# A two-layer trunk on one core: the FFN's down product summed in PSUM, and a unit's decays and first low-rank stage put behind the preceding unit's inversion

## The chip, the cores and the metric

The kernel runs on one core of a Trainium2 chip. The metric is the device time of one execution in microseconds (us). A core has engines that run their own instruction streams: TensorE (PE) for matrix products, VectorE (DVE), ScalarE (ACT) and GpSimd (POOL) for elementwise work, and SyncE (SP), which here issues the transfers (DMAs) between HBM and on-chip memory. PE writes its results to PSUM, of which the kernel uses eight banks of 128x512 fp32 numbers; the other engines read them there.

## The reference, cut to what matters

The program is a trunk of two layers over 1024 tokens of width 1024, all in float32. Each layer has a mixer and a gated FFN, both with a residual and a LayerNorm after it. The mixer of layer 0 is RWKV-7, a recurrence over time; that of layer 1 is sparse attention (called dsa in the code).

```python
def _wkv7_step(state, inp):
    r_t, w_t, k_t, v_t, a_t, b_t = inp
    sa = jnp.einsum('bhvk,bhk->bhv', state, a_t)
    state = (state * w_t[:, :, None, :] + sa[..., None] * b_t[:, :, None, :]
             + v_t[..., None] * k_t[:, :, None, :])
    y = jnp.einsum('bhvk,bhk->bhv', state, r_t)
    return state, y
...
w_log = -jax.nn.softplus(-(w0 + jnp.tanh(xw @ w1) @ w2)) - 0.5      # low-rank
decay = jnp.exp(-jnp.exp(w_log.astype(f32)))
a = jax.nn.sigmoid(a0 + (xa @ a1) @ a2)                              # low-rank
g = jax.nn.sigmoid(xg @ g1) @ g2                                     # low-rank
...
def conv_ffn(x, w_up, conv_w, conv_b, w_down):
    u = x @ w_up                                                     # 1024 -> 5632
    up = jnp.pad(u, ((0, 0), (CONV_W - 1, 0), (0, 0)))
    u = sum(up[:, j:j + S] * conv_w[j] for j in range(CONV_W)) + conv_b
    gate, val = jnp.split(u, 2, axis=-1)
    return (jax.nn.silu(gate) * val) @ w_down                        # 2816 -> 1024
...
for i in range(DEPTH):
    ...
    x = layer_norm(DN_ALPHA * x + h, ln_g[i, 0], ln_b[i, 0])
    f = conv_ffn(x, ffn_w_up[i], ffn_conv_w[i], ffn_conv_b[i], ffn_w_down[i])
    x = layer_norm(DN_ALPHA * x + f, ln_g[i, 1], ln_b[i, 1])
```

## The kernel before, in words

A float32 product is made of three matmuls on rounded operands (mm3, lines 65 to 67): each operand is split into a high part, which ACT casts (line 54), and a low part, the rest, which DVE or POOL subtracts (line 60). High by high, low by high and high by low are summed in the same PSUM bank.

The program runs in five stretches: the RWKV mixer (to about 960 us), the FFN of layer 0 (its up product to 1437.8 us, its down product to 1733 us, where dsa's first transposes begin), dsa (to about 2430 us), and the FFN of layer 1 (up to 2893.1 us, down to the end at 3168.0 us). A scheduler places each instruction on its engine's stream from the order in which the code issues it and from when its inputs come ready; `tc.issue_after(i)` keeps the instructions issued inside it behind instruction `i` on that instruction's own engine.

**RWKV.** There are four units (hf, g): token half hf and head half g, units 0 to 3. For each unit the stages are low-rank products (lora1 at line 401, once for each hf, and lora2 at 497), projections (kproj, rproj, vproj; PSUM tiles "pa"), decays (510), prep (603), bonus (579), the inversion of the chunks' triangular matrices (invert, 630) and the recurrence over eight chunks (wkv, 695). In the inversion DVE runs a chain of 30 steps on the tile Lt, each a product (line 644, into ltmp) and a sum (line 650), and then transposes the result (lines 655 and 660), on which PE works (lines 667 and 672). In wkv every chunk goes round PE (ups at 718, dps at 724) and DVE (the copy UV at 719, the state S at 727), so that a chunk waits for the one before. `CFG['order']` is a list of stages with an offset: x is the loading of the next token half with lora1, l lora2, d decays, b bonus, i invert, w and W the first and second four chunks, and the digit says how many units ahead. Decays are, for each of four head pairs, one scan (520), one difference (521) and one product on DVE (527), and some work on ACT and POOL. lora1 is, for each of eight k tiles, a difference (406) and three scaled sums on DVE (413), and four matmuls.

**The down product.** It multiplies hd (2816 features by 1024 tokens, stored in HBM by the gating) by w_down (2816 by 1024). The features are cut into 22 tiles f of 128, in 11 pairs p. Of the first 20 features (layer 0) or 18 (layer 1) the product is made by Strassen's and Winograd's scheme: token halves, column halves and the two f of a pair are the 2x2 blocks, and seven products (`11`, `12`, `S1`, `S2`, `S3`, `S4`, `22`) take the place of eight. Pairs are taken in groups (`cuts`, 4 in layer 0, 3 in layer 1): d_load brings hd and w_down of a group's pairs, d_op makes the sums of operands on DVE (lines 908 and 1147) and splits them (dh, dl; 128x1024 at a time), `down` makes the 128x512 products for four token tiles tt, summed in PSUM over a group's pairs, and add_to (line 1166) adds each bank to the sums acc in SBUF, on DVE. The last two f (layer 0) or four (layer 1) are the "tail": a direct product "dt" (line 1260) for each token tile and column half, added to acc, after which norm_store normalizes the tile's rows and stores them. In layer 0 dsa's first steps are interleaved with the tail: two blocks of 32 small matmuls (wqk, line 1326), the stores of what ACT and POOL make of them, and the loads of x for dsa's transposes (line 1357).

Of the kernel before, what the change touches and what calls it, by code (L numbers as in the profile page):

```python
# [300 lines left out]
CFG = {'order': 'k0 r0 a0 A0 v0 x1 l0 l1 x0 d0 b0 i0 w0 W0 r1 d1', 'da': 'p', 'db': 'p', 'kk': 'p', 'uv': 'a', 'go': 'v', 'gz': 'p', 'wr': 'pppv', 'wk': 'vp', 'wv': 'pv', 'xl': 'ppp', 'xp': 'vppppppp', 'p1': 'q0 w q5 i4 t1 at i5', 'n1': 27, 'n2a': 26, 'n2b': 19, 'n3': 20, 'n4': 12, 'qp': 2, 'lag': 2, 'cm': 'pppp', 'phc': 'aaaa', 'olc': 'a', 'qm': 'av', 'quq': 'p', 'quk': 'v', 'sh': 16, 'tc': 'a', 'kve': 'a', 'cB': 'a', 'cU': 'a', 'cY': 'a', 'cV': 'aaaa', 'cR': 'aaaa', 'cT': 'a', 'cM': 'a', 'cUV': 'v', 'sq': 'a', 'kkE': 'a', 'pfl': 'n', 'l2': 'v', 'l1': 'v', 'wo0': 'vppvppvp', 'wl': 'ppvv', 'wl2': 'v', 'wl3': 'vv', 'gz2': 'v', 'yq': 'a', 'pfo': 0, 'pf0': 0, 'pf1': 1, 'pf2': 2, 'dwo0': 'pppppppp', 'dwl': 'vvvv', 'dwl2': 'v', 'dwl3': 'vv', 'tke': 'av', 'rt': 'f2 l0 z f0 f1 p0 p2 l1 f3 p1 p3 p4 l2 l4 l5 l3', 'dt': 'l0 a z l1 p0 p4 p2 p3 p1 l5 l2 l3 l4', 'eT1': 'pvpvvvpv', 'eT3': 'pvpvpppv', 'fs0': 'x0 x1 y1 y0 x2 y2 x3 y3 r0 r1 u0 r3 u3 r2 u4 u6 u2 u7 u5 u1', 'fs1': 'x0 y0 x1 x3 y1 x2 y2 r0 u0 y3 r1 r2 u1 r3 u3 u4 u2 u5 u6 u7', 'eT2': 'vvvvvvvv', 'e22': 'vvvvvvvv', 'eR': 'vvvvvvvv', 'tkp': 'vv', 'kvs': 1, 'ln0': 'pp', 'ln1': 'vv', 'ln2': 'pppppppv', 'ln3': 'pppppppv', 'ln4': ['pp', 'pp'], 'gl': 2, 'ga': '0g1g', 'dl0': 'pppppvppp'}  # L301
# [5 lines left out]
def rwkv(k, src, dst):  # L307
# [201 lines left out]

    def decays(hf, g):  # L510
# [4 lines left out]
        with tc.issue_after(s["last"].ins):  # L515
# [114 lines left out]
    def invert(hf, g):  # L630
# [21 lines left out]
        for sub in range(2):  # L652
# [5 lines left out]
            for b in range(2):  # L658
                q = slice(64 + 32 * b, 96 + 32 * b)
                nc.vector.transpose(  # L660
                    L[q, :, 32 * b : 32 * b + 32].rearrange("p n i -> p i n"),
                    Lt[64 * sub + 32 * b : 64 * sub + 32 * b + 32],
                )
            for o in (0, 16):
# [172 lines left out]
    def stage(n, i):  # L837
# [3 lines left out]
        if n == "x":  # L841
            if un_[1] == 0:
                load_x(un_[0])
                lora1(un_[0])
# [39 lines left out]
def ffn(k, layer, src, dst):  # L884
# [239 lines left out]
    NPAIR = NF // 2  # L1124
    cuts = [0, 3, 6, 8, 10] if layer == 0 else [0, 3, 6, 9]
    groups = [range(a, b) for a, b in zip(cuts, cuts[1:])]
# [849 lines left out]
```

## The time and the profile before

| | |
|---|---|
| time before, median of 3 runs | 3173.01 us (3172.37 to 3178.31) |
| the profiled execution's own time | 3170.01 us |
| its span in the profile | 3168.0 us |
| PE busy | 2834.0 us (89%) |
| DVE busy | 2463.5 us (78%) |
| POOL busy / ACT busy | 1528.7 us (48%) / 1368.9 us (43%) |
| granted PE clock, mean | 0.937 |

A row of grouped instructions has line, engine, operation, output and inputs, shape and count, then busy time and the mean of one, then the engine's idle time just before them and what ended it. A row of the timeline has start, duration, engine, line, operation and count, and in brackets the idle time before it with what ended it. A matmul's duration there (0.39 us) is its latency; matmuls follow each other faster than that. The view by windows gives for a stretch the busy time of PE, PE's weight loads, DVE, ACT and POOL with their counts, the granted PE clock (1.00 is full), the busy share of the DMA engines and GB/s.

### The profile page before, as it was taken

The page shows a single profiled execution, that of the slowest core. Times are in us where ns is not written, and L with a number is a line of the kernel's source. Part 1 is how long each engine was busy: PE and PEld are TensorE (multiplying, and loading weights), DVE is VectorE, ACT ScalarE, POOL GpSimd, SP SyncE. Part 2 cuts the span into 40 slices and gives each one's busy share as a digit, 9 for nine tenths or more (in the row PEclk, how much of TensorE's full clock was granted, in tenths as well). Part 3 has the DMA queues.
Part 4 walks back from the last instruction along what each step waited for, and adds up shares of the span by engine and source line. Part 5 has one row for each costly group of instructions (what it writes and reads, how often), then busy time and mean ns, then how long its engine had stood idle before and what let it go on. Part 6 is the DMA issues. An engine that isn't in the chain of part 4 may idle for free. (4 is left out here: it accounts for less than half of the span.)

```text
span 3168.0 us, 41686 instructions
## 1 busy us (share of the span) xinstructions
PE 2834.0 (89%) x15032; PEld 2217.4 (70%) x15032; DVE 2463.5 (78%) x3911; ACT 1368.9 (43%) x2353; POOL 1528.7 (48%) x987
## 2 busy tenths in 40 slices
PE   7789998898988999997888888889998899998798
PEld 3577576786866777775667765667776677777577
DVE  6776776768576888889786699995675888888965
ACT  4433243322233544443224487784363444444231
POOL 3525045140246666666677222212214666666766
PEclk9889998898998999998998989899999999999899
DMA  6645435344162222244115221113224222225212
GB/s 214 246 152 195 142 121 199 134 148 146 64 201 89 80 80 80 80 143 189 41 40 173 102 90 37 34 40 115 77 66 151 60 80 80 80 81 206 80 53 93
DMA packets 235232, 354.87 MB, mean 112 GB/s; under 512 B 17194, under 2 KB 110762, under 8 KB 234642
## 3 DMA queue, kind: packets, MB, share of 16 engines
q1 hardware_dynamic: 221202, 327.04, 31.6%
q10 hardware_dynamic: 13824, 25.17, 2.2%
q8 instruction: 118, 1.93, 0.3%
q14 instruction: 88, 0.72, 0.1%
HBM read 248.99 MB, written 103.15 MB: 111 GB/s over the span
## 5 line engine op out<-in xcount | busy, mean ns | idle before, releaser
L60 POOL TENSOR_TENSOR wo<-wr,wo 128x512 fp32r<-128x512 f32 x220 | 414.3, 1907 | 289.4 <-ACT wo L54 289.4
L1039 DVE SCALAR_TENSOR_TENSOR cv<-u,vec,cv 128x1023 f32<-128x1023 f32 (+1 forms) x176 | 348.0, 1995 | 52.9 <-ACT cv L1034 51.2
L65 PE MATMUL dn<-dh 128*128 128x512 f32 x532 | 220.3, 414 | 67.8 <-DVE acc L1166 67.8
L60 POOL TENSOR_TENSOR dl<-raw,dh 128x1024 fp32r<-128x1024 f32 x82 | 220.2, 2708 | 102.2 <-ACT dh L54 96.7
L65 PE MATMUL p<-xT,wo 128*128 128x512 f32 x528 | 213.1, 404 | 27.8 <-ACT u L1023 18.2
L66 PE MATMUL dn<-dl,dh 128*128 128x512 f32 x532 | 218.1, 410 | 14.3 <-DVE dl L60 7.5
L1671 POOL TENSOR_TENSOR cm<-sc,toep 128x256 f32<-128x256 f32 x96 | 75.7, 795 | 298.1 <-DVE mn L1687 229.7
L1034 ACT ACTIVATE cv<-u,vec 128x1024 f32<-128x1024 f32 x88 | 109.5, 1244 | 250.2 <-DVE u L1028 249.6
L67 PE MATMUL dn<-dh,dl 128*128 128x512 f32 x532 | 217.0, 408 | 0.0
L67 PE MATMUL p<-xT,wo 128*128 128x512 f32 x528 | 208.8, 395 | 2.9 <-POOL wo L60 2.9
L66 PE MATMUL p<-xT,wo 128*128 128x512 f32 x528 | 208.5, 395 | 3.0 <-DVE xT L60 3.0
L1166 DVE SCALAR_TENSOR_TENSOR acc<-acc,dn 128x512 f32<-128x512 f32 x196 | 131.0, 680 | 86.3 <-PE dn L67 86.3
L60 POOL TENSOR_TENSOR wo<-S,wo 128x512 fp32r<-128x512 f32 x88 | 173.3, 1987 | 30.0 <-ACT wo L54 25.7
L54 ACT CAST dh<-raw 128x1024 fp32r<-128x1024 f32 x95 | 94.8, 1047 | 199.6 <-issue 81.1
L65 PEld LDWEIGHTS dn<-dh 128*128 128x128 f32 x532 | 106.3, 200 | 98.5 <-DVE acc L1166 42.2
L60 POOL TENSOR_TENSOR wl<-wr,wh 128x512 fp32r<-128x512 f32 x56 | 76.3, 1363 | 181.7 <-ACT wh L54 109.1
L65 PEld LDWEIGHTS p<-xT,wo 128*128 128x128 f32 x528 | 100.7, 191 | 65.4 <-ACT u L1023 33.0
L65 PE MATMUL p<-x,wo 128*128 128x512 f32 x352 | 138.9, 394 | 3.4 <-DVE x L60 3.0
L54 ACT CAST wo<-wr 128x512 fp32r<-128x512 f32 x220 | 127.2, 619 | 27.3 <-POOL wo L60 18.6
L67 PE MATMUL p<-x,wo 128*128 128x512 f32 x352 | 138.4, 393 | 0.0
L66 PE MATMUL p<-x,wo 128*128 128x512 f32 x352 | 138.4, 393 | 0.0
L66 PEld LDWEIGHTS dn<-dl,dh 128*128 128x128 f32 x532 | 106.5, 200 | 38.4 <-DVE dl L60 8.4
(412 smaller groups left out, 8552.0 us busy)
## 6 DMA issues: line engine op xcount, KB each, us to landing
wr<-in_w_up_dram SPq DMA_DIRECT2D x88, 512.0 KB, 5.9
hd<-cv SPq DMA_DIRECT2D x44, 512.0 KB, 3.4
raw<-hd SPq DMA_DIRECT2D x19, 1024.0 KB, 5.0
raw<-in_w_down_dram SPq DMA_DIRECT2D x19, 1024.0 KB, 7.6
wr<-in_w_wo_dram SPq DMA_DIRECT2D x68, 256.0 KB, 2.9
wr<-in_w_rkv_dram SPq DMA_DIRECT2D x48, 256.0 KB, 4.3
kept_w<-wh ACTq DMA_DIRECT2D x48, 256.0 KB, 3.5
kept_w<-wl SPq DMA_DIRECT2D x48, 256.0 KB, 3.0
```

What stands on the lines that cost most here:

```text
L54: nc.scalar.copy(hi, raw)
L60: eng.tensor_tensor(lo, raw, f32(hi), ALU.subtract)
L65: mm(ps, lhs[0], rhs[0], start=start, stop=False, **kw)
L66: mm(ps, lhs[0], rhs[1], start=False, stop=False, **kw)
L67: mm(ps, lhs[1], rhs[0], start=False, stop=stop, **kw)
L1034: nc.scalar.activation(o, u, AF.Identity, bias=k.vec[:, cb : cb + 1], scale=k.vec[:, cw[2] : cw[2] + 1])
L1039: nc.vector.scalar_tensor_tensor(o[:, d:], u[:, : 1024 - d], k.vec[:, cw[j] : cw[j] + 1], o[:, d:], ALU.mult, ALU.add)
L1166: nc.vector.scalar_tensor_tensor(o, o, ALPHA if first else 1.0, ps, ALU.mult, ALU.add)
L1671: (nc.vector if CFG["cm"][h4] == "v" else nc.gpsimd).tensor_tensor(cm[:, :near], mk, toep[g][:, h % 8, 256 - near :], ALU.add)
```

## The change

The **down product** becomes a direct one. It runs over two token halves hf and eleven pairs p in 22 steps. d_prep of a step loads the half's 512 tokens of hd for the pair (hr, 512 KB) and both rows of w_down (dr, 2 x 512 KB), and splits them: three 128x1024 casts on ACT, the low part of hd on DVE (on POOL in the second half of layer 1 for four pairs), both low parts of w_down on POOL. It is issued two steps ahead. A step has 48 matmuls: two f, three products, four token tiles, two column halves. All eight banks of a half stay open over its eleven pairs; the last two pairs are done bank by bank in d_end, with one addition of the bank to the residual rows on DVE, and after it d_norm. w_down is read and split for each half. The Strassen products, their operand sums, the 196 additions of banks to acc (111 of them in layer 0) and the tail product are gone. d_norm of the first half lies in the middle of the product; in layer 0 dsa's first steps are interleaved with d_end of the second half.

The **recurrence** changes in its order only: in `CFG['order']` x1 and l1 stand behind i0, not ahead of l0, and decays and lora1 are issued inside `tc.issue_after` of the last transpose of the first half of the preceding unit's inversion. What is computed there is the same.

```diff
-CFG = {'order': 'k0 r0 a0 A0 v0 x1 l0 l1 x0 d0 b0 i0 w0 W0 r1 d1',
+CFG = {'order': 'k0 r0 a0 A0 v0 l0 x0 d0 b0 i0 x1 l1 w0 W0 r1 d1',
...
+    inverted = []
+
     def decays(hf, g):
...
-        with tc.issue_after(s["last"].ins):
+        with tc.issue_after(s["last"].ins), tc.issue_after(inverted[-1].ins) if inverted else nullcontext():
...
-                nc.vector.transpose(
+                tr = nc.vector.transpose(
                     L[q, :, 32 * b : 32 * b + 32].rearrange("p n i -> p i n"),
                     Lt[64 * sub + 32 * b : 64 * sub + 32 * b + 32],
                 )
+            if sub == 0:
+                inverted.append(tr)
...
-                lora1(un_[0])
+                with tc.issue_after(inverted[-1].ins) if inverted else nullcontext():
+                    lora1(un_[0])
...
+    NPAIR, LAST = NF // 2, 2
+    ops, hold, lnw, sums, rows = {}, {}, [], {}, {}
+
+    def d_prep(hf, p):
+        late = hf == 1 and p >= NPAIR - LAST
+        hr = t4("hr")
+        nc.sync.dma_start(
+            hr.rearrange("p (f c) -> p f c", f=2), hd[p][:, :, 512 * hf : 512 * hf + 512].rearrange("f p c -> p f c")
+        )
...
+        split(k, hr, *h, "a", "p" if layer and hf and p < 4 else "v")
+        for f in range(2):
+            wr = t4("dr", pool=N_)
+            nc.sync.dma_start(wr, k.w_down[layer, (2 * p + f) * 128 : (2 * p + f + 1) * 128, :])
+            split(k, wr, w[:, 2 * f], w[:, 2 * f + 1], "a", "p")
+        ops[hf, p] = *h, w
+
+    def d_mm(ps, hf, p, tt, ch):
+        hh, hl, w = ops[hf, p]
+        for f in range(2):
+            ts = slice(512 * f + 128 * tt, 512 * f + 128 * tt + 128)
+            cs = slice(512 * ch, 512 * ch + 512)
             mm3(
+                k, ps, (hh[:, ts], hl[:, ts]), (w[:, 2 * f, cs], w[:, 2 * f + 1, cs]), p == f == 0,
+                p == NPAIR - 1 and f == 1,
             )
+
+    def d_end(ps, hf, tt, ch):
+        for p in range(NPAIR - LAST, NPAIR):
+            d_mm(ps, hf, p, tt, ch)
...
+        nc.vector.scalar_tensor_tensor(
+            r, r, ALPHA, ps, ALU.mult, ALU.add, accum_out=sums[hf, tt][:, ch : ch + 1]
+        )
+
+    def d_norm(hf, tt):
...
+    steps = [(hf, p) for hf in range(2) for p in range(NPAIR)]
+    for s in steps[:2]:
+        d_prep(*s)
+    for f in range(NF - CFG["gl"], NF):
+        gated(f)
+    order = [(ch, tt) for ch in (1, 0) for tt in range(4)]
+    for i, (hf, p) in enumerate(steps):
+        if i + 2 < len(steps):
+            d_prep(*steps[i + 2])
+        if p == 0:
+            bk = {x: bank("dn", PX if x[0] == 0 else PY) for x in order}
+        if p < NPAIR - LAST:
+            for ch, tt in order:
+                d_mm(bk[ch, tt], hf, p, tt, ch)
...
+        if (hf, p) == (0, NPAIR - 1):
+            for ch, tt in order:
+                d_end(bk[ch, tt], 0, tt, ch)
+                if ch == 0:
+                    d_norm(0, tt)
+    for tt in range(4):
+        d_end(bk[1, tt], 1, tt, 1)
     if layer == 0:
         pools.close(P_, N_, PY)
         yield
...
+    for tt in range(4):
+        d_end(bk[0, tt], 1, tt, 0)
+        d_norm(1, tt)
         if layer == 0:
             yield
```

The streams show three places that the diff does not. The first is DVE in the inversion of unit 0, in the second half of the chain on Lt. Before, rows of decays (520, 521, 527) and a low part of a weight (wl) stand between the steps:

```order
L644 TENSOR_TENSOR ltmp<-Lt 128x220
L650 TENSOR_TENSOR Lt<-Lt,ltmp 128x11x20
L520 SCALAR_TENSOR_TENSOR c<-smask,BK 128x512
L644 TENSOR_TENSOR ltmp<-Lt 128x210
L60 TENSOR_TENSOR wl<-wr,wh 128x512
L650 TENSOR_TENSOR Lt<-Lt,ltmp 128x10x21
L521 TENSOR_TENSOR d<-c,BK 128x512
L644 TENSOR_TENSOR ltmp<-Lt 128x198
L650 TENSOR_TENSOR Lt<-Lt,ltmp 128x9x22
L527 TENSOR_TENSOR BK<-AR,ip 128x8x64
```

In the changed kernel (where 644, 650, 655, 660 and 719 of before are 647, 653, 658, 663 and 724) the chain's steps stand alone up to the transposes, and the decays follow:

```order
L647 TENSOR_TENSOR ltmp<-Lt 128x30
L653 TENSOR_TENSOR Lt<-Lt,ltmp 128x30
L658 STREAM_TRANSPOSE TX<-Lt 32x32x32
L663 STREAM_TRANSPOSE MA<-Lt 32x32x32 x3
L658 STREAM_TRANSPOSE TX<-Lt 32x32x32
L663 STREAM_TRANSPOSE MA<-Lt 32x32x32
L523 SCALAR_TENSOR_TENSOR c<-smask,BK 128x512
L524 TENSOR_TENSOR d<-c,BK 128x512
L724 COPY UV<-ups 64x512
```

So the twelve DVE instructions of the unit's decays moved from between the chain's steps to between the steps of wkv's chunks; the first copy UV of wkv has two of them ahead of it. Unit 2 reads the same.

The second place is DVE in unit 1, where lora1 of the second token half stood in the middle of the chain (ahead of its step on 128x238). Of the changed kernel:

```order
L663 STREAM_TRANSPOSE MA<-Lt 32x32x32
L406 TENSOR_TENSOR xx<-xT 128x512 x2
L413 SCALAR_TENSOR_TENSOR xm<-xx,vec,xT 128x512 x6
L406 TENSOR_TENSOR xx<-xT 128x512 x2
L413 SCALAR_TENSOR_TENSOR xm<-xx,vec,xT 128x512 x6
L406 TENSOR_TENSOR xx<-xT 128x512 x2
L413 SCALAR_TENSOR_TENSOR xm<-xx,vec,xT 128x512 x6
L406 TENSOR_TENSOR xx<-xT 128x512 x2
L413 SCALAR_TENSOR_TENSOR xm<-xx,vec,xT 128x512 x6
L724 COPY UV<-ups 64x512
```

All 32 instructions of lora1 now stand behind the inversion and ahead of the first copy UV of the unit's recurrence, and on PE the matmuls of lora1 stand between ups and dps of that first chunk.

The third place is the end of layer 0's down product, on SP and PE. On SP (x_4 to x_6 are stores of normalized rows, wqkh and wqkl those of wqk, xr the loads of x for dsa's transposes) the changed kernel has, with rows that repeat left out:

```order
L1295 DMA wqk<-wqkh 128x512
L1295 DMA wqk<-wqkl 128x512
L1280 DMA uk<-in_w_uk_dram 128x512
L149 DMA x_4_78<-acc 128x512 x2
L149 DMA x_5_79<-acc 128x512
L149 DMA x_6_80<-acc 128x512
L1304 DMA grow<-in_dsa_rows_dram 128x512
L1271 DMA xr<-x_0_74 128x512 x2
```

Eight stores of wqk stand ahead of the second load of uk, the other eight between x_4 and grow, all ahead of the loads xr. Before, SP had these kinds in the same order, with the rows x_0 to x_2 where x_4 to x_6 are now. What moved is the work of PE beside them. Where PE had these rows around its second block of wqk before,

```order
L67 MATMUL dt<-to 128x512
L1326 MATMUL wqk<-uk,uq 128x128 x16
L65 MATMUL dt<-to 128x512
L66 MATMUL dt<-to 128x512
```

it now has

```order
L66 MATMUL dn<-wd,hl 128x512
L1287 MATMUL wqk<-uk,uq 128x128 x16
L67 MATMUL dn<-wd,hl 128x512
L65 MATMUL dn<-wd,hl 128x512
```

Between the two blocks of wqk stood 45 matmuls and stand 34; between the second block and dsa's transposes stood 39 and stand 10.

More of the change, by code (lines that the diff above doesn't have):

```diff
@@ L1121, in ffn @@
             gated(f)
-    NPAIR = NF // 2
-    cuts = [0, 3, 6, 8, 10] if layer == 0 else [0, 3, 6, 9]
-    groups = [range(a, b) for a, b in zip(cuts, cuts[1:])]
-    in_P = (0, 3, 4, 8, 9) if layer == 0 else (0, 3, 6, 8)
-    tail = range(2 * cuts[-1], NF)
-    acc = []
-    R = {}
-    def d_load(p):
-        r = R[p] = dict(raw=big("raw", P_ if p in in_P else L_, (128, 8, 512), F32))
-        raw = r["raw"]
-        nc.sync.dma_start(raw[:, 0:4].rearrange("p (f a) c -> p f (a c)", f=2), hd[p].rearrange("f p c -> p f c"))
+    NPAIR, LAST = NF // 2, 2
@@ L1204, in ffn @@
-    hs = []
-    def tail_op(f):
-        if layer == 1 and f == NF - 1:
-            room = [t4("to", F32R, N_) for _ in range(4)]
-        else:
-            room = big("to", L_, (128, 4, 1024))
-            room = [room[:, i] for i in range(4)]
-        for i, ap in enumerate((hd[f // 2][f % 2], k.w_down[layer, f * 128 : (f + 1) * 128, :])):
-            raw = t4("tr")
-            nc.sync.dma_start(raw, ap)
-            split(k, raw, room[2 * i], room[2 * i + 1], "a", "p")
-        hs.append(room)
@@ L1238, in ffn @@
-    if len(tail) > 3:
-        tail_op(tail[3])
-    lnw = []
-    for z in range(2):
-        if layer == 0:
-            lnw.append(L_.tile([128, D], F32, name=f"lnw{z}"))
-        else:
-            lnw.append(sm("lnw").rearrange("p a b -> p (a b)"))
-        i = B_LN + 4 * layer + 2 + z
-        nc.sync.dma_start(lnw[z], k.bvec[i : i + 1, :].to_broadcast([128, D]))
+            hr.rearrange("p (f c) -> p f c", f=2), hd[p][:, :, 512 * hf : 512 * hf + 512].rearrange("f p c -> p f c")
+        )
@@ new lines, in d_norm @@
+    def d_norm(hf, tt):
+        r = [rows[hf][:, tt, 512 * ch : 512 * ch + 512] for ch in range(2)]
+        kw = {} if layer else dict(
+            sums=sums[hf, tt], junk=L_.tile([128, 512], BF16, name="lnj", tag="lnj", bufs=1)
+        )
+        norm_store(
+            k, L_, r, lnw, dst, 128 * (4 * hf + tt), CFG["ln4"][layer] if (hf, tt) != (1, 3) else "pv", **kw
+        )
+    steps = [(hf, p) for hf in range(2) for p in range(NPAIR)]
[3 more added lines that the diff above has]
+        gated(f)
@@ L1250, in ffn @@
         yield
[L1251 to L1264 removed]
+        for tt in range(4):
+            yield
+    for tt in range(4):
+        d_end(bk[0, tt], 1, tt, 0)
+        d_norm(1, tt)
         if layer == 0:
```

112 lines of the change are left out of this document (22 added, 90 removed).

## The prediction

> **What bounds the kernel now.** The whole page says PE 89% busy, but the change touches four stretches with different limits, so I read the windows first: an undisturbed part of the up product for comparison, then for each layer the Strassen part and the tail of the down product. The columns are the window, its length, busy time of PE, PE's weight loads, DVE, ACT and POOL with counts, the granted clock, the DMA share and GB/s.
>
> ```profile
> 1100.00:1390.00 290.00, 282.15 (x1228) 228.80 (x1226) 252.69 (x178) 135.97 (x208) 200.86 (x103) 1.00 0.30 82
> 1437.80:1692.50 254.70, 207.81 (x841) 165.99 (x840) 201.09 (x186) 73.60 (x74) 173.24 (x66) 0.90 0.20 75
> 1692.50:1733.00 40.50, 33.41 (x162) 26.98 (x161) 30.17 (x67) 25.53 (x53) 30.20 (x25) 0.91 0.64 215
> 2893.10:3114.50 221.40, 186.22 (x754) 149.98 (x753) 174.06 (x154) 70.23 (x71) 156.74 (x60) 0.90 0.23 86
> 3114.50:3168.00 53.50, 44.39 (x196) 36.41 (x194) 37.77 (x90) 6.54 (x8) 29.15 (x24) 0.95 0.21 79
> ```
>
> In the up product the clock is full and PE is busy 97%; in the down product PE is busy 82% to 84% at a clock of 0.90, while DVE and POOL are busy 68% to 79%. So there it isn't PE alone that sets the time. The groups by line of layer 0's Strassen part say who ends PE's idle time:
>
> ```profile
> L65 PE MATMUL dn<-dh 128*128 128x512 f32 x280 | 115.5, 413 | 38.2 <-DVE acc L1166 38.2
> L66 PE MATMUL dn<-dl,dh 128*128 128x512 f32 x280 | 114.8, 410 | 8.7 <-DVE dl L60 4.6 <-POOL dl L60 4.1
> L60 POOL TENSOR_TENSOR dl<-raw,dh 128x1024 fp32r<-128x1024 f32 x42 | 112.8, 2708 | 51.9 <-ACT dh L54 51.9
> L1166 DVE SCALAR_TENSOR_TENSOR acc<-acc,dn 128x512 f32<-128x512 f32 x111 | 74.3, 680 | 43.8 <-PE dn L67 43.8
> ```
>
> PE waits 38.2 us for additions on DVE that free banks (or for what stands behind them), and 8.7 us for low parts. The time of a matmul at full clock comes from PE's timeline in an undisturbed stretch, from its first and last row (56 matmul starts apart):
>
> ```profile
> 3039.64 0.39 PE L67 MATMUL dn<-dh,dl 128*128 128x512 f32 x1
> ...
> 3052.33 0.39 PE L66 MATMUL dn<-dl,dh 128*128 128x512 f32 x1
> ```
>
> That is 12.69 / 56 = 0.2267 us per matmul. Behind a long wait they are slower:
>
> ```profile
> 1497.84 0.79 PE L65 MATMUL dn<-dh 128*128 128x512 f32 x1 [13.24 <-DVE acc L1166]
> 1498.43 0.63 PE L66 MATMUL dn<-dl,dh 128*128 128x512 f32 x1
> ...
> 1503.12 0.61 PE L65 MATMUL dn<-dh 128*128 128x512 f32 x1
> ```
>
> Eleven starts in 4.69 us are 0.426 each; the thirteen slow matmuls cost about 13 x 0.2 = 2.6 us beyond the wait itself. Layer 0's 840 matmuls would take 840 x 0.2267 = 190.4 us; the window is 254.7, so 64.3 us are waits and slow clock.
>
> **The down product, part by part.** The count of matmuls goes up. Seven products for four token tiles of three matmuls are 84 per pair; with the tail's 96 and 192 before had 840 + 96 in layer 0 and 756 + 192 in layer 1, 1884 in all. Now 22 steps of 48 are 1056 per layer. At full clock that is 1056 x 0.2267 = 239.4 us per layer, 27.2 and 24.5 us more than the old counts need. What goes against it is the waits. Out go the operand sums and 111 additions in layer 0's window (and 83 in layer 1's); a bank is now read by DVE once per half, 16 additions per layer. What feeds a step is 1.5 MB of loads, three casts and two low parts on POOL. The prices are these (the cast and the two POOL rows from the group view of layer 0's window, the loads from the list of DMA issues with KB and median us to landing):
>
> ```profile
> L54 ACT CAST dh<-raw 128x1024 fp32r<-128x1024 f32 x45 | 44.9, 1047 | 108.8 <-issue 59.0 <-PE dn L67 35.6 <-DMA raw<-in_w_down_dram 6.7
> L60 POOL TENSOR_TENSOR to<-tr,to 128x1024 fp32r<-128x1024 f32 x4 | 9.6, 2402 | 0.0
> ...
> wr<-in_w_up_dram SPq DMA_DIRECT2D x88, 512.0 KB, 5.9
> ```
>
> POOL needs 2 x 2.4 to 2 x 2.7 = 4.8 to 5.4 us a step, ACT 3.1, and PE takes 48 x 0.2267 = 10.9 us, so POOL is busy half the time, and with two steps issued ahead a chain of 5.9 + 1.05 + 5.4 = 12.4 us has about 21.8 us of cover. The loads are 22 x 1.57 MB = 34.6 MB in 239 us, 145 GB/s; the row of 1692.5 to 1733 shows 215. So I cost the supply at nothing, hidden by PE; without that cover it is the first rival. The start of a half (first low parts, a bank held by an addition) I put at 3 us per layer; bounds 0 and 13.2 (the long wait above).
>
> *End of layer 0.* I count from 1437.8 to dsa's first transpose, 295.2 us. These rows of PE and SP show what stands there:
>
> ```profile
> 1695.52 3.50 PE L1326 MATMUL wqk<-uk,uq 64*128 64x128 f32 x32
> 1713.86 5.24 PE L1326 MATMUL wqk<-uk,uq 64*128 64x128 f32 x32 [3.62 <-DMA uk<-in_w_uk_dram]
> 1733.00 1.94 PE L1357 MATMUL pt<-ident,xr 128*128 128x128 f32 x8 [3.42 <-DMA xr<-x]
> ...
> 1729.79 0.32 SPq L1334 DMA_DIRECT2D wqk<-wqkl  x1
> 1730.16 2.81 SPq L1310 DMA_DIRECT2D xr<-x  x6
> ```
>
> From the first wqk block to the transposes are 37.5 us, paced by low parts on POOL, stores on SP behind them and then the loads. With 34 matmuls between the blocks and 10 behind them, PE has 3.5 + 7.7 + 5.2 + 2.3 = 18.7 us of work in that stretch. If the chain of stores keeps its length, PE waits 18.8 us; if it shrinks under PE's work, none. POOL now has the norms of four token tiles there, not of eight, so I take 12 us, and one slow start of 2.7. The sum is 239.4 + 3 + 8.7 (wqk) + 12 + 2.7 = 265.8, against 295.2: **-29 us**, between -44 (no waits) and -10.
>
> *End of layer 1.* The window from 2893.1 to 3168.0 is 274.9 us. The last rows of DVE are
>
> ```profile
> 3158.93 0.69 DVE L1260 SCALAR_TENSOR_TENSOR acc<-acc,dt 128x512 f32<-128x512 f32 x1 [0.33 <-PE dt L67]
> 3164.27 0.69 DVE L111 TENSOR_TENSOR acc<-acc,lnw 128x512 f32<-128x512 f32 x1 [1.56 <-POOL acc L110]
> ```
>
> The last matmul ends where the first row starts, 9.1 us before the end. A token tile came every 24 x 0.2267 = 5.4 us and its norm kept up. Now a tile of the last half comes every 12 x 0.2267 = 2.7 us, and the norm (an addition and two statistics, five short ones and two of 0.74, some 4.3 us of DVE, and POOL beside it) lags by 1.6 to 2.3 us a tile, over three tiles 5 to 7. I take 9.1 + 6 = 15. The sum is 239.4 + 3 + 15 = 257.4: **-17 us**, between -27 (nothing lost at start and no lag) and -4 (a wait of 13.2 at a start).
>
> **The clock.** The slow rows stand behind the 13.24 us wait, and the up product, with the same matmul and hardly a wait, has 1.00. I conclude that the 0.90 is a consequence of the waits and goes with them. The Trainium skill, "TensorE: Matmul & The Clock Gate", section "What's actually happening", has the same rule: half clock after an idle window of about 3.4 us, full again after about 3.4 us of work. By it a slow start costs 1.7 us, and the sum would be 1 us less; the row shows 4.7 us at the slow pace and more, so this trace doesn't agree on the size, and I keep the row's.
>
> **The recurrence.** These rows of DVE are unit 0's inversion (first step, the two steps on 128x220 that lie either side of the middle, a scan of decays, the transpose that ends it), and then unit 2's scan and transpose:
>
> ```profile
> 170.08 0.21 DVE L644 TENSOR_TENSOR ltmp<-Lt 128x30 f32<-128x30 f32 x1
> 177.83 0.39 DVE L644 TENSOR_TENSOR ltmp<-Lt 128x220 f32<-128x220 f32 x1
> 182.13 1.21 DVE L520 TENSOR_TENSOR_SCAN c<-smask,BK 128x512 f32<-128x512 f32 x1
> 188.96 1.47 DVE L644 TENSOR_TENSOR ltmp<-Lt 128x220 f32<-128x220 f32 x1
> 208.17 1.92 DVE L655 STREAM_TRANSPOSE TX<-Lt 32x1024 f32<-32x1024 f32 x1
> ...
> 583.99 1.22 DVE L520 TENSOR_TENSOR_SCAN c<-smask,BK 128x512 f32<-128x512 f32 x1
> 609.79 1.90 DVE L655 STREAM_TRANSPOSE TX<-Lt 32x1024 f32<-32x1024 f32 x1
> ```
>
> The chain's first half takes 12.1 us (170.08 to 182.13), the second, which mirrors it but has decays between, 26.0; unit 2's second half 25.8. Without the decays the transposes come 13 us earlier in each. But the decays don't vanish: they now stand between chunks of wkv, where the copies UV show what that costs:
>
> ```profile
> L719 DVE COPY UV<-ups x8: 694/694/695, 234.7 to 294.1; 64x512 f32<-64x512 f32 x8
> ...
>   PE ups L718: 22.9, 7
> ...
> L719 DVE COPY UV<-ups x8: 694/694/696, 429.6 to 495.5; 64x512 f32<-64x512 f32 x8
> ```
>
> Eight chunks with five instructions of decays among them took 59.4 us in unit 0, and 65.9 in unit 1 with sixteen and nine of other work: 6.5 us for twenty more, so 5 to 6 us for the twelve that come. The projections that PE did during the longer inversion are left for later: behind wkv stand 7 matmuls more in unit 0 and 15 in unit 2, 1.6 and 3.4 us. Unit 0 is then -13 + 5.5 + 1.6 = -6, unit 2 -13 + 5.5 + 3.4 = -4.
>
> In unit 1 lora1 stood inside the chain:
>
> ```profile
> 361.83 1.28 DVE L406 TENSOR_TENSOR xx<-xT 128x512 f32<-128x512 f32 x2
> 382.55 0.40 DVE L644 TENSOR_TENSOR ltmp<-Lt 128x238 f32<-128x238 f32 x1
> 429.60 0.69 DVE L719 COPY UV<-ups 64x512 f32<-64x512 f32 x1 [2.70 <-PE ups L718]
> ```
>
> Its 20.7 us move behind the inversion, ahead of the first UV, which therefore comes about when it did. On PE 20 matmuls of projections are left behind wkv, 4.5 us, where lora1's were. I take +4. Together the recurrence is -6 - 4 + 4 = **-6 us**, bounds -26 (both gains of 13 kept) and +21 (unit 1 pays the 20.7 in full and the others gain nothing).
>
> **The sum** is -29 - 17 - 6 = -52 us on the profiled execution's own 3170.0 (2.0 us lie around its span), 3118. The median of the runs is 3 us above that execution, so I predict 3121.
>
> **Rivals.** *The supply is serial (slower).* If the buffers of the loads let only one step's chain run at a time, a step takes 5.9 + 1.05 + 5.4 = 12.4 us, not 10.9, and the 44 steps cost 44 x 1.5 = 66 us more: 3187. It decides above 10.9 + 52/44 = 12.1 us a step. For it: POOL's low part at 2708 ns is the longest link, and w_down is now read twice. Against: two steps of cover, and the 215 GB/s. The Trainium skill, "GPSIMD Engine Reference", section "1. Specifications", says that POOL contends with DVE instructions of two SBUF inputs; by it the low part would fall toward 2402 ns now that DVE has few, the step to 11.8 us and the loss to 38 us, which is no longer slower than before. The rows of 2402 and 2708, seen under different loads of DVE, do not contradict it.
>
> *The clock belongs to the down product (no change).* At 0.90, 1056 matmuls take 266 us a layer, 53 us more in all: 3174. For it: both windows show 0.90. Against: the 1.00 of the up product.
>
> *The recurrence keeps all it gains (faster still).* If decays and lora1 hide wholly between chunks, units 0 and 2 give 13 each and unit 1 17 (its 20.7 less the 4 above): -43, not -6: 3084. For it: in unit 0 DVE waits 22.9 us for ups, at seven of eight chunks, more than the twelve instructions need. Against: a chunk waits on both engines in turn, and the first UV of unit 1 stands behind all 32 instructions.
>
> **How the numbers follow.** My forecast has a chance of 0.77, the serial supply 0.07, the clock 0.05, the recurrence 0.11. The bounds of the terms (-44 to -10, -27 to -4, -26 to +21) hardly fall together. The root of the sum of their squares is 27 us below the forecast (15, 10 and 20) and 35 above (19, 13 and 27): 3094 to 3156 for the forecast itself. To leave no more than 2 in 10 outside, the range reaches below to the last rival: 3082 to 3156. A difference of 0.2%, 6 us, is about what can be told from none here. Faster by more has 0.77 + 0.11 = 0.88, within it 0.05, slower 0.07.
>
> **What would show it right or wrong.** The down product of each layer should have a clock near 1.00, PE waits of a few us only at its start, its middle and its end, and about 240 us of matmuls; waits of L65 or L66 for POOL's low parts or for loads at every step would speak for the serial supply, a clock of 0.90 without waits for the second rival. In layer 0 the wait for xr should grow from 3.4 to about 10 us. In units 0 and 2 the first transpose of Lt should come 13 us earlier after the chain's first step, and the copies UV spread over some 65 us; in unit 1 the first UV should come about where it was, and if it comes more than 10 us later, or earlier, the term of the recurrence is wrong.

## The result and the profile after

The changed kernel takes 3134.0 us (median of 4 runs, 3131.7 to 3136.2) where the kernel before took 3175.7 beside it (4 runs, 3172.4 to 3185.3): a ratio of 0.9864, interval 0.984 to 0.9888. In a later set of runs the two gave 0.9844 (0.9816 to 0.9871). The forecast was 3121 in a range of 3082 to 3156. The profiled run took 3131.7, its span is 3129.9.

The view by windows of the changed kernel, in the columns of before: part of the up product of layer 0, then for each layer the down product up to its last steps and the stretch behind.

```profile
1116.00:1406.00 290.00, 281.89 (x1226) 228.63 (x1225) 252.47 (x178) 135.94 (x207) 201.06 (x103) 1.00 0.30 82
1453.40:1682.80 229.40, 229.40 (x1013) 189.82 (x1012) 74.28 (x78) 78.55 (x92) 122.01 (x57) 1.00 0.48 168
1682.80:1718.60 35.80, 17.52 (x109) 14.71 (x108) 15.24 (x37) 19.48 (x39) 23.93 (x21) 0.83 0.59 206
2874.40:3066.00 191.60, 191.60 (x847) 158.63 (x846) 69.55 (x69) 67.71 (x69) 124.28 (x54) 1.00 0.54 198
3066.00:3129.90 63.90, 47.99 (x212) 39.41 (x210) 18.52 (x45) 5.26 (x6) 17.86 (x13) 0.89 0.09 33
```

PE is busy all of the 229.4 and the 191.6 us, at full clock. In layer 0 DVE falls from 79% of the time to 32%, POOL from 68% to 53%. The groups by line on the page say the same: of the kernel before, the row of L65 has 67.8 us of idle time before it (first row); of the changed kernel, the three rows that hold 1984 of the 2112 matmuls have none. The other 128, of the last two pairs of the second half in each layer, have none either.

```profile
L65 PE MATMUL dn<-dh 128*128 128x512 f32 x532 | 220.3, 414 | 67.8 <-DVE acc L1166 67.8
...
L60 POOL TENSOR_TENSOR wd<-dr,wd 128x1024 fp32r<-128x1024 f32 x88 | 224.8, 2582 | 134.9 <-ACT wd L54 134.9
L67 PE MATMUL dn<-wd,hl 128*128 128x512 f32 x704 | 274.0, 389 | 0.0
L65 PE MATMUL dn<-wd,hh 128*128 128x512 f32 x640 | 249.0, 389 | 0.0
L66 PE MATMUL dn<-wd,hh 128*128 128x512 f32 x640 | 249.0, 389 | 0.0
```

Where the 38.1 us between the two spans lie can be read from a few marks of PE's timelines: the "first up matmul", the end of that product, dsa's first transpose, the end of layer 1's up product, the end. The "first up matmul" is, here and in the expectations below, the first row `p<-xT,wo` of layer 0's up product; the first 15 or 16 us of that product, on other operands, stand ahead of it in every profile.

| stretch | before | after | difference |
|---|---|---|---|
| to the first up matmul (the recurrence) | 1001.1 | 1016.5 | +15.4 |
| the rest of layer 0's up product | 436.7 | 436.9 | +0.2 |
| down product of layer 0, to dsa's transposes | 295.2 | 265.2 | -30.0 |
| dsa and up product of layer 1 | 1160.1 | 1155.8 | -4.3 |
| down product of layer 1, to the end | 274.9 | 255.5 | -19.4 |

The two down products gave 49.4 us. The recurrence, forecast at -6, ends 15.4 us later in this pair of profiles. That is the question for the runs.

### The profile page after: what moved, and what is told of

Same layout as the page of the kernel before. It is cut to its first block, busy times and chain, and to the rows that moved or that the text cites. A ratio compares the mean times of both kernels' runs of the same rounds, so it can differ in the third digit from the quotient of the medians.

```text
span 3129.9 us, 41844 instructions
## 1 busy us (share of the span) xinstructions
PE 2852.7 (91%) x15260; PEld 2249.3 (72%) x15260; DVE 2161.4 (69%) x3609; ACT 1358.0 (43%) x2340; POOL 1406.9 (45%) x947
## 5 line engine op out<-in xcount | busy, mean ns | idle before, releaser
L60 POOL TENSOR_TENSOR wd<-dr,wd 128x1024 fp32r<-128x1024 f32 x88 | 224.8, 2582 | 134.9 <-ACT wd L54 134.9
L67 PE MATMUL dn<-wd,hl 128*128 128x512 f32 x704 | 274.0, 389 | 0.0
L65 PE MATMUL dn<-wd,hh 128*128 128x512 f32 x640 | 249.0, 389 | 0.0
L66 PE MATMUL dn<-wd,hh 128*128 128x512 f32 x640 | 249.0, 389 | 0.0
L65 PE MATMUL p<-xT,wo 128*128 128x512 f32 x528 | 213.3, 404 | 25.7 <-ACT u L1029 19.3
L60 DVE TENSOR_TENSOR hl<-hr,hh 128x1024 fp32r<-128x1024 f32 x36 | 57.6, 1601 | 160.5 <-ACT hh L54 100.0
L67 PEld LDWEIGHTS dn<-wd,hl 128*128 128x128 f32 x704 | 132.2, 188 | 27.5
L65 PEld LDWEIGHTS p<-xT,wo 128*128 128x128 f32 x528 | 100.5, 190 | 63.9 <-ACT u L1029 34.5
L65 PE MATMUL p<-x,wo 128*128 128x512 f32 x352 | 138.5, 394 | 2.9 <-DVE x L60 2.5
L54 ACT CAST wd<-dr 128x1024 fp32r<-128x1024 f32 x88 | 89.3, 1050 | 115.2 <-DMA dr<-in_w_down_dram 51.1
L65 PEld LDWEIGHTS dn<-wd,hh 128*128 128x128 f32 x640 | 120.1, 188 | 25.1
L66 PE MATMUL p<-x,wo 128*128 128x512 f32 x352 | 137.9, 392 | 0.0
L66 PEld LDWEIGHTS dn<-wd,hh 128*128 128x128 f32 x640 | 120.1, 188 | 24.7
```

Of the source, the lines that this page charges most:

```text
L54: nc.scalar.copy(hi, raw)
L60: eng.tensor_tensor(lo, raw, f32(hi), ALU.subtract)
L65: mm(ps, lhs[0], rhs[0], start=start, stop=False, **kw)
L66: mm(ps, lhs[0], rhs[1], start=False, stop=False, **kw)
L67: mm(ps, lhs[1], rhs[0], start=False, stop=stop, **kw)
```

## The experiments

Each of these is the changed kernel with an edit, but for the one that starts from the kernel before. Times are medians; "ratio" is to the kernel before, run beside it on the same chip (medians there 3182 to 3186).

**The down product alone.**

```diff
-CFG = {'order': 'k0 r0 a0 A0 v0 l0 x0 d0 b0 i0 x1 l1 w0 W0 r1 d1',
+CFG = {'order': 'k0 r0 a0 A0 v0 x1 l0 l1 x0 d0 b0 i0 w0 W0 r1 d1',
...
-        with tc.issue_after(s["last"].ins), tc.issue_after(inverted[-1].ins) if inverted else nullcontext():
+        with tc.issue_after(s["last"].ins):
...
-                with tc.issue_after(inverted[-1].ins) if inverted else nullcontext():
-                    lora1(un_[0])
+                lora1(un_[0])
```

> The new down product alone, with the order of the recurrence as before (CFG order as before, decays and lora1 not tied to the inversion). In the trace of the changed kernel the recurrence ends 15.4 us later than before (first up matmul at 1016.5, not 1001.1), layer 0 from the end of up to dsa's first transpose takes 265.4 and not 295.2, layer 1 from the end of up to the end 255.6 and not 274.9, and dsa 4.4 less. Theory A, the recurrence's new order costs that time: this kernel comes out at the changed kernel's 3134 less 15, 3119 (3113 to 3124), and its first up matmul is at about 1001. Theory B, the new down product itself shifts the recurrence, since pools and scheduling are shared: 3134 within 3, and the first up matmul at about 1016.

Measured: 3129.2 (4 runs, 3115.8 to 3146.8), ratio 0.9838 (0.9787 to 0.989). Its profiled run took 3135.2, and its first up matmul is at 1019.4. Neither theory fits: until some 30 us before the end of the up product the instructions of PE, DVE, POOL and SP stand in the order of before, and still the recurrence took 18 us longer than in the profile of before. Windows from 50 to 350 us of the kernel before and then of this one show PE as busy as before, with 30 matmuls fewer done, at a lower granted clock:

```profile
50.00:350.00 300.00, 261.78 (x1830) 206.07 (x1829) 220.57 (x298) 123.94 (x209) 134.94 (x105) 0.91 0.60 209
```

```profile
50.00:350.00 300.00, 262.82 (x1800) 206.55 (x1799) 213.12 (x287) 123.32 (x208) 133.08 (x103) 0.87 0.60 204
```

Whether the lower clock made the stretch longer, or longer waits lowered the clock, these rows don't say. So one pair of profiles can't give the price of the recurrence's order. The stretches behind it can be trusted: up to dsa's transposes 265.0 us here, layer 1 255.7.

**The recurrence's order alone**, on the kernel before (the added lines of the diff's first part, nothing of the down product).

> The recurrence's new order alone, with the down product of before. Theory A: 15 us slower than before, 3190 (3184 to 3196), first up matmul at about 1016. Theory B: within 3 us of before. The forecast's own term was 6 us faster, 3169.

Measured: 3187.0 (10 runs, 3182.2 to 3197.5), ratio 1.0016 (0.9997 to 1.0036): 1 us faster to 11 slower, near 5. It is not the 6 us of gain that were forecast, and not 15 us of loss. Its layer 0 shows 295.1 us from up to the transposes, the value of before.

**Decays tied, lora1 as before**, and **lora1 tied with the new list, decays as before**, both with the new down product:

```diff
# first
-CFG = {'order': 'k0 r0 a0 A0 v0 l0 x0 d0 b0 i0 x1 l1 w0 W0 r1 d1',
+CFG = {'order': 'k0 r0 a0 A0 v0 x1 l0 l1 x0 d0 b0 i0 w0 W0 r1 d1',
...
-                with tc.issue_after(inverted[-1].ins) if inverted else nullcontext():
-                    lora1(un_[0])
+                lora1(un_[0])
# second
-        with tc.issue_after(s["last"].ins), tc.issue_after(inverted[-1].ins) if inverted else nullcontext():
+        with tc.issue_after(s["last"].ins):
```

> New down product, and of the recurrence's change only the decays behind the preding unit's inversion; lora1 and the order of stages as before. Against the run with the down product alone: theory A1, the cost lies in lora1 and lora2, whose 80 matmuls (31 us) now stand between ups and dps of unit 1's first chunk: decays alone change it by -6 to +3 (their 13 us out of units 0 and 2 come back between the chunks). Theory A2, the cost is the decays', which delay each following unit: +8 to +15. The first copy UV of unit 1 should come within some us of before's distance from the last of unit 0 (135 us) under A1.

> New down product, and of the recurrence's change only lora1 behind the inversion with the new order of stages; decays as before. Against the run with the down product alone: theory A1 (lora1 and lora2 on PE between ups and dps of the first chunk of unit 1): +9 to +16, with unit 1 taking the whole of it (PE idle about 15 us in its inversion, and the second UV 25 us behind the first). Theory A2 (the decays cost it): within 4.

Measured: decays alone 3124.0 (4 runs, 3117.8 to 3130.5), ratio 0.9812; lora1 alone 3137.2 (4 runs, 3133.4 to 3138.6), ratio 0.9858. Beside the 3129.2 of the down product alone that is -5 and +8, with runs that spread over 31 us.

The profiles bear out the signs of A1 only in part. With lora1 alone PE waits 15.7 us in unit 1's inversion and the second UV comes 25.6 us behind the first, as expected; but unit 1 doesn't take the whole of the cost, since its length from the first chain step to the last UV stays (149.3 us, where the profiles with the old order have 147 to 152). With decays alone the first UV of unit 1 comes 161.5 us behind the last of unit 0, not some 135, and unit 1 is 18 us longer; the stretch behind it is 6 us shorter and unit 2's inversion 13. A second profile of that kernel has the same 161.7. So to move the decays is not harmless in unit 1, though the time of the whole kernel shows no loss; DVE has longer waits there ahead of the first UV (the longest 8.5 us for ups, 2.7 before), and why was not tried.

The comparison was repeated on one chip with the changed kernel:

> The changed kernel once more, beside the next three on one chip. The run of the recurrence's order alone was 4 us (0.16%, interval -0.03% to 0.36%) above the kernel before, and the trace of the down product alone, whose instructions in the recurrence stand word for word as before on every engine, still ended the recurrence 18 us later at a granted clock of 0.87, not 0.91, over 50 to 350 us: so executions of one and the same stream differ there by more than the effect. Theory C: the recurrence's new order costs little (0 to +9 us) and the changed kernel lies that much above the down product alone. Theory A of the first runs: 15 us above it.

> The down product alone, again, for the difference from the changed kernel on one chip: theory C 0 to 9 us faster than the changed kernel, theory A 12 us or more. Its recurrence should show a clock between 0.86 and 0.92 over 50 to 350 us, and the sooner it ends, the higher the clock.

> Down product and decays behind the inversion, lora1 as before, again. In the first call it was 8 us faster than the down product alone (ratios 0.9812 and 0.9838 with intervals that overlap). If the decays' move is worth its 6 to 10 us, it is again 5 us or more below the down product alone; if that was noise, within 4.

Measured: the changed kernel 3135.1 (5 runs, 3125.9 to 3141.3), the down product alone 3122.2 (4 runs, 3121.1 to 3125.6), decays tied 3125.0 (5 runs, 3117.5 to 3133.9). In this set the changed kernel is 13 us above the down product alone by medians, 11.5 by means: more than theory C allowed (9), and near theory A's mark of 12. The clock of the down product alone was 0.90, inside what was expected, but it does not order the profiles as expected: of kernels with the old order, one with 0.90 ended the recurrence at 1018.1 us and one with 0.87 at 1013.0. Both sets together have the down product alone at a mean of 3126.5 (8 runs), decays at 3125.3 (9), lora1 tied at 3136.6 (4) and the changed kernel at 3134.3 (5). The decays' move is worth nothing that can be told (-1 us, with a 95% interval of 9 either way), lora1's costs about 10 (8 either way), and both together 8 (9 either way). More runs give a clearer answer. Of those with the new down product and dsa as in the changed kernel (the next experiment's too, the loaded supply's not), 13 with lora1 tied have a mean of 3134.9 and 23 without it 3126.6: 8 us, interval 5 to 12, with decays tied or not in both groups.

The place in unit 1 is plain in the timelines of PE and then DVE of the changed kernel (first transpose of the inversion, the matmuls of lora1, dps; the first and second copy UV):

```profile
386.50 3.62 PE L672 MATMUL xps<-TX,MA 32*32 32x32 f32 x64 [15.82 <-DVE TX L658]
...
407.50 1.97 PE L723 MATMUL ups<-U,MA 64*64 64x64 f32 x16
...
409.87 25.80 PE L418 MATMUL la<-xm,wl 128*64 128x512 f32 x63
...
436.66 0.56 PE L729 MATMUL dps<-UV,B 128*64 128x64 f32 x10
```

```profile
422.95 0.69 DVE L724 COPY UV<-ups 64x512 f32<-64x512 f32 x1
...
448.57 0.69 DVE L724 COPY UV<-ups 64x512 f32<-64x512 f32 x1 [2.78 <-PE ups L723]
```

Before, lora1's matmuls filled PE during the inversion. Now PE waits 15.8 us there, and the first chunk's dps stands behind 25.8 us of them: the second UV follows the first by 25.6 us, where the down product alone has 8.7.

**lora1 untied**, with the new list and tied decays:

```diff
-                with tc.issue_after(inverted[-1].ins) if inverted else nullcontext():
-                    lora1(un_[0])
+                lora1(un_[0])
```

> The changed kernel, with decays behind the inversion and the new list of stages, but lora1 not tied. DVE's and PE's streams then have lora1 and lora2 inside unit 1's inversion again. If their place behind the inversion is what the recurrence's change costs: PE's wait of 15.8 us for the first transpose in unit 1 falls below 6 us, ups to dps of the first chunk falls from 29 us to under 5, and the kernel is 6 to 12 us faster than the changed one (ratio to the kernel before 0.981 to 0.983, not 0.9844 to 0.9864). If the new list of stages or the decays cost it, it stays at the changed kernel's time.

Measured: 3128.8 (6 runs, 3124.1 to 3132.8; mean 3128.6), ratio 0.9822 (0.9788 to 0.9857), by means 5.7 us below the changed kernel. PE has no wait for the first transpose in unit 1 any more, and from ups to dps are 2.0 us:

```profile
404.49 2.31 PE L672 MATMUL xps<-TX,MA 32*32 32x32 f32 x64
...
433.53 1.22 PE L723 MATMUL ups<-U,MA 64*64 64x64 f32 x16
...
435.57 0.69 PE L729 MATMUL dps<-UV,B 128*64 128x64 f32 x16
```

That PE's wait and the late dps come from lora1's place is shown. The size is less sure: 5.7 us lie just under what was expected, and the two ratios' intervals overlap. Other costs of the order stay (table below).

**The wqk stores out of the way of the loads of x**, on the down product alone. The second half of wqk is issued in dsa's loop, behind the loads of four token tiles:

```diff
-    for h4 in range(2):
+    def wqk_half(h4):
...
+    wqk_half(0)
...
     for tt in range(8):
+        if tt == 4:
+            wqk_half(1)
         x_load(tt)
```

> The down product alone, and in dsa the second half of wqk (16 products, 8 low parts, 8 stores, one load) is issued behind the loads of the first four token tiles of x, not ahead of them. In the changed kernel PE waits 17.3 us for xr at the end of layer 0, because the loads stand in SP's queue behind the stores of wqk, which wait for POOL. If that queue is the cause: the wait falls below 4 us, and the kernel is 10 to 17 us faster than the down product alone. If it is the norm of the last rows or a buffer that holds the loads back, the wait stays above 12 us and the time within 4 us.

Measured: 3120.8 (5 runs, 3115.1 to 3123.7), ratio 0.9796 (0.9767 to 0.9825), 1.4 us below the down product alone and not 10 to 17. The wait itself did what the queue explains: these are PE's first transpose and SP's last store of wqk ahead of the loads, of the changed kernel, and then the transpose of this one.

```profile
1718.64 2.58 PE L1318 MATMUL pt<-ident,xr 128*128 128x128 f32 x11 [17.30 <-DMA xr<-x]
...
1712.25 0.32 SPq L1295 DMA_DIRECT2D wqk<-wqkl  x1
...
1713.11 9.52 SPq L1271 DMA_DIRECT2D xr<-x  x10
```

```profile
1699.67 0.63 PE L1319 MATMUL pt<-ident,xr 128*128 128x128 f32 x4 [3.19 <-DMA xr<-x]
```

The wait fell to 3.2 us (17.3 in the changed kernel, 16.8 in the down product alone), and from the end of one up product to the end of the next it is 1411.0 us, not 1419.5 (down product alone): 8.5 us gained, part of the 14 being paid back later in dsa, into which seven of the down product's last matmuls and the second half of wqk have moved. In the whole run little of it can be told, because this profile's recurrence ended at 1018.1 and that of the down product alone at 1008.6.

**The tail of layer 1**, on top of that:

```diff
-    for tt in range(4):
+    for tt in range(4 if layer == 0 else 0):
         d_end(bk[1, tt], 1, tt, 1)
...
     for tt in range(4):
+        if layer == 1:
+            d_end(bk[1, tt], 1, tt, 1)
         d_end(bk[0, tt], 1, tt, 0)
```

> The kernel with the late half of wqk, and in layer 1 the last half's banks ended tile by tile (both column halves of a token tile one after the other, then its norm), not all first column halves ahead of all second ones. The forecast put the end behind the last matmul at 15 us since norms come every 2.7 us and lag; the changed kernel shows 15.9. With a tile every 5.4 us the lag should go: 9 to 11 us from the last matmul's end to the end, layer 1 from the end of up 250 us (255.6 without), and the kernel 5 us faster than the one with late wqk alone. If the end is not the norms' lag but the last tile's own chain, it stays at 15 to 16.

Measured: 3113.3 (6 runs, 3110.5 to 3125.3), ratio 0.9783 (0.975 to 0.9815), the lowest median of all; beside the 3120.8 with late wqk alone the runs don't separate the two, the stretch does. The last matmul and the last row of DVE, of the changed kernel and then of this one:

```profile
3113.61 0.39 PE L67 MATMUL dn<-wd,hl 128*128 128x512 f32 x1
...
3126.13 0.69 DVE L111 TENSOR_TENSOR acc<-acc,lnw 128x512 f32<-128x512 f32 x1 [1.56 <-POOL acc L110]
```

```profile
3099.21 0.39 PE L67 MATMUL dn<-wd,hl 128*128 128x512 f32 x1
...
3104.97 0.69 DVE L111 TENSOR_TENSOR acc<-acc,lnw 128x512 f32<-128x512 f32 x1 [1.56 <-POOL acc L110]
```

From the last matmul's end to the end of the span are 15.9 us in the changed kernel (3114.0 to 3129.9) and 9.1 here (3099.6 to 3108.7): the norms' lag was the cause, and layer 1 takes 248.9 us, not 255.5.

**The supply, loaded further**, on the down product alone: each low part of w_down is made twice, and then three times, on POOL (the later ones write the same numbers).

```diff
             split(k, wr, w[:, 2 * f], w[:, 2 * f + 1], "a", "p")
+            nc.gpsimd.tensor_tensor(w[:, 2 * f + 1], wr, f32(w[:, 2 * f]), ALU.subtract)
```

> The down product alone, with each low part of w_down made twice on POOL (the second writes the same numbers). Of the profile of the down product alone: POOL 2551 to 2614 ns a low part, so a step's four take 10.2 to 10.5 us beside 10.9 us of matmuls, and the whole chain of a step (load 3.7, cast 1.05, 10.4) is 15.2 us. If only the busiest engine of a step counts (two steps of cover): hidden but for the starts, from the end of up to dsa's first transpose 265 to 275 us (264.9 without) and layer 1 256 to 268, clock 1.00 and PE waits of under 10 us in the steps together. The first rival's serial supply would give 22 x (15.2 - 10.9) = 95 us more in each layer.

> The same with each low part made three times: POOL 15.3 to 15.7 us a step, over the 10.9 us of matmuls. Then POOL sets the pace: 22 x (15.5 - 10.9) = 101 us more in each layer, PE waits about 4.6 us at each step for POOL's wd. If slow clock follows waits, the granted clock in the down product, 1.00 without this, falls to 0.75 to 0.9 though the matmuls are the same, and the slow matmuls themselves are hidden in the waits; if the clock had belonged to the kind of matmul it stays at 1.00.

Measured: twice 3217.6 (2 runs), three times 3400.9 (2 runs). Layer 0 from up to the transposes takes 316.1 and 404.5 us (264.9 without), layer 1 299.8 and 388.2 (255.7 without): +51 and +44, then +140 and +133. The windows of the three kernels' layer 0 (down product alone, twice, three times), with the low part of hd on DVE in the first, and the group of PE that waits in the others:

```profile
1445.30:1674.00 228.70, 228.70 (x1010) 189.38 (x1009) 74.50 (x77) 78.30 (x92) 122.48 (x57) 1.00 0.49 168
...
L60 DVE TENSOR_TENSOR hl<-hr,hh 128x1024 fp32r<-128x1024 f32 x18 | 30.7, 1704 | 82.4 <-PE dn L66 44.9 <-ACT hh L54 37.5
```

```profile
1446.00:1725.00 279.00, 247.50 (x1011) 197.94 (x1010) 101.81 (x77) 78.94 (x93) 241.13 (x100) 0.94 0.40 140
...
L66 PE MATMUL dn<-wd,hh 128*128 128x512 f32 x320 | 132.6, 414 | 31.1 <-POOL wd L1153 31.1
...
L1153 POOL TENSOR_TENSOR wd<-dr,wd 128x1024 fp32r<-128x1024 f32 x43 | 119.7, 2800 | 0.7
L60 DVE TENSOR_TENSOR hl<-hr,hh 128x1024 fp32r<-128x1024 f32 x18 | 42.2, 2343 | 84.4 <-ACT hh L54 84.4
```

```profile
1446.50:1814.00 367.50, 271.67 (x1010) 208.96 (x1009) 100.57 (x76) 78.34 (x92) 344.37 (x143) 0.84 0.31 106
...
L66 PE MATMUL dn<-wd,hh 128*128 128x512 f32 x320 | 143.2, 447 | 95.8 <-POOL wd L1154 95.8
```

The expectation for twice was wrong: it isn't hidden. Of layer 0's 51 us, 31 are PE's waits for the second low part and 19 are slower matmuls (PE is busy 247.5 us with them, 228.7 without). POOL's pieces fill 241 of 279 us, the second low part takes 2800 ns and DVE's hl beside them 2343 (1704 without), and POOL does its norms in between. That this makes it a second bound beside PE is how I read it, not shown apart; it is not the serial chain (95 us). With three POOL is busy 94% and sets the pace. There too the expectation (101 us) was 32 to 39 us too low: it counted the low parts and not POOL's other work and its own waits. And the same matmuls that had a clock of 1.00 get 0.94 and 0.84 with waits between them: the clock follows the waits. The Trainium skill ("TensorE: Matmul & The Clock Gate", section "What's actually happening") says too that the clock is set by how busy PE has been recently. It puts the loss of the full clock behind an idle window of about 3.4 us; with the low parts made twice, waits of 1.5 and 1.9 us, which end at 1474.5 and 1501.0 us, are followed by some 3 us at a clock of 0.50 too.

## Why the prediction was right or wrong

The time lies in the range and the main part was right; the total came out 10 us too good (-52 forecast, -42 measured). One term had the wrong sign, the recurrence, which missed by 11 to 15 us (-6 forecast; 5 to 9 us of loss found); that the total missed by less is luck, since the down products gave 3 us more than forecast and the stretch of dsa 4 that nobody forecast.

**Layer 0, forecast -29, measured -30.0.** The steps hold: 1056 matmuls at 0.2267, the clock at 1.00, additions off the path. Start and middle of the product, put at 3 us, cost nothing. The wait for xr was sized at 12 with 18.8 as the bound if the chain of stores keeps its length; it was 17.3 (and 1.0 for uk), so the bound was the better value: POOL did fewer norms there, but the later ones stand between wqk's low parts and their stores. That the sum is right to 1 us is therefore partly luck: the wait was 6 us longer with that for uk, and the start, the middle and the slow start, put at 5.7 together, didn't show.

**Layer 1, forecast -17, measured -19.4.** No waits at the start (3 forecast), 15.9 us behind the last matmul (15 forecast), for the reason given.

**The clock.** It went with the waits, as argued, and the loaded runs show it in the other direction too. The second rival is out.

**The supply at nothing.** Right for this kernel: PE never waited. But the margin was overstated. "POOL is busy half the time" was right (122 of 229 us); that a step has two steps of cover does not mean that POOL could take twice the work, as the run with doubled low parts showed. The rule cited there from the Trainium skill ("GPSIMD Engine Reference", section "1. Specifications": contention with DVE instructions of two SBUF inputs) agrees with these traces: DVE's 1704 ns became 2343 as POOL filled up, and POOL's low part, 2708 before, took 2582 with DVE less busy, though not the 2402 that the forecast drew from it.

**The recurrence, forecast -6: the step that failed.** In runs, the order alone costs 5 us (-1 to 11) on the kernel before and 8 (-2 to 17) on the new one (means of 8 and 5 runs). For the pieces I take means over profiles, from PE's and DVE's timelines, since one profile isn't enough: 7 with the old order (before and the runs with its order) and 3 with the new (changed kernel twice, order alone).

| stretch (mean us) | old order | new order | difference | forecast |
|---|---|---|---|---|
| unit 0: first chain step to transpose of Lt | 38.1 | 28.2 | -9.9 | -13 |
| unit 0: first to last UV | 60.1 | 66.7 | +6.6 | +5.5 |
| unit 0: last UV to unit 1's first chain step | 55.6 | 63.4 | +7.8 | +1.6 |
| unit 1: first chain step to last UV | 149.8 | 147.9 | -1.9 | about 0 |
| unit 1: last UV to unit 2's first chain step | 73.4 | 82.7 | +9.3 | +4 |
| unit 2: first chain step to transpose of Lt | 36.8 | 24.8 | -12.0 | -13 |
| unit 2: first to last UV | 60.6 | 64.5 | +3.9 | +5.5 |
| unit 2: last UV to unit 3's first chain step | 53.2 | 58.6 | +5.4 | +3.4 |

These pieces make +9.2 us together, and -6 were forecast. In six of the eight rows (not unit 1's length and not the last) the two orders' profiles don't overlap. From the span's start to the first up matmul the means differ by 13.8 us; of the 4.6 outside the table 3.1 lie ahead of unit 0's inversion, where the streams are the same, so that much is spread. The gain in the chain and its return between the chunks were forecast within 3.1 us each. What was missed is the stretch *between* units: +22.5 us in all where 9 were forecast. The windows of that stretch behind unit 0, of before and then of the changed kernel, show why; the third row is that of lora1 untied:

```profile
294.10:347.40 53.30, 50.08 (x336) 39.37 (x337) 38.67 (x52) 15.78 (x27) 17.07 (x12) 1.00 0.62 210
```

```profile
295.30:358.10 62.80, 59.48 (x358) 47.34 (x359) 43.33 (x57) 15.97 (x27) 16.93 (x12) 0.92 0.62 205
```

```profile
297.30:357.00 59.70, 55.07 (x358) 43.53 (x359) 43.36 (x57) 15.97 (x27) 16.98 (x12) 1.00 0.66 216
```

PE is busy 94% and 95% of it in the first two, with 22 matmuls more (PE's timelines have 125 projections there, 103 before; behind unit 1 171 and 151, behind unit 2 123 and 110). The forecast had 7, 20 and 15 left over and priced all of them at 0.2267 each. The first number was a third of the true one, and the price was low: 7.8, 9.3 and 5.4 us for 22, 20 and 13 matmuls are 0.35 to 0.47 us each. Part of it is a lower clock: with lora1 untied the stretch behind unit 0 has the same 22 matmuls more at 1.00, as before, and takes 6.4 us more than before, 0.29 each. What the rest is, the runs don't say. The point behind it: a chain on DVE was cover for work on PE. A shorter chain does not shorten PE's work, and PE is the busiest engine of the stretch that follows. Slips of the front part and the forecast belong here. The decays in unit 0's inversion are those of unit 1, not its own. They are sixteen instructions on DVE, not twelve, with a second product for each head pair (AR<-AR,c); of these, eight more than before come to stand among unit 0's chunks and nine more among unit 2's. And unit 1's chunks had 11 DVE instructions more among them than unit 0's (77 and 66), not twenty. That the price of 5.5 us came near 6.6 and 3.9 is therefore partly luck.

In unit 1 the forecast had the first UV "about when it did", and lora1 on PE at nothing but the projections it displaces. The first UV came 6.7 us earlier in the span (422.9, not 429.6), and counted from unit 1's own first chain step 17.4 us earlier (64.8 us, 82.2 before), since the chain got 35 us shorter and 18 of them came back between its transpose and the first UV, where lora1 now stands. The missed price is the 25.8 us of lora1's matmuls between ups and dps: from the first UV to the second are 25.6 us, where 8.6 were. That takes the 17 us back, which is why the unit's own length stays (147.9 and 149.8), right as forecast but not for its reason, while its gain, on which the third rival rested, is gone. That rival is refuted.

**Not forecast:** some 4 us less in dsa and layer 1's up product, in the eight profiles with the new down product, its supply not loaded and dsa unchanged (1154.6 to 1156.8, and 1158.8 and 1160.1 with the old one). About 2.5 of it lie right at dsa's start, where the first transposes to the first projection take 3.3 us and took 5.8, with more rows of x loaded; for the rest no cause was tried.

## What to carry to other kernels

Fewer multiplications are no gain where PE then waits for the operand sums and the additions of results on other engines: here 228 more matmuls, nearly all back to back at full clock in open PSUM banks, took 49 us less than the seven-product scheme with its waits. When work is moved out of a long chain on one engine, ask what another engine did under that chain: it will do it afterwards, and in a recurrence a stage moved "behind" one wait lands ahead of the next. And where executions of one stream differ by more than the effect, split the span at marks and compare the stretches, over several profiles.

## What the runs showed of the hardware

The same instruction streams ended the recurrence at 1001 to 1019 us in seven profiles, with a granted clock of 0.87 to 0.91 from 50 to 350 us; a stretch full of short waits has a time of its own in each execution, while a down product without waits repeated within 1 us (264.7 to 265.4 from the end of up to dsa's transposes in eight profiles). And the low-part subtractions of DVE and POOL lengthen each other. DVE's (128x1024) took 1704 ns on average with POOL 54% busy and 2343 with POOL 86% busy. Sorted by what POOL did beside them, in the profile of the down product alone, 14 with POOL idle took 1.21 to 1.23 us and nine with POOL busy throughout 1.46 to 3.43; POOL's own took 2.39 to 2.42 us with DVE idle and up to 3.40 with DVE busy beside them.
